# Down projection with four output tiles side by side, gated tiles loaded in pairs, residual loaded later

## The chip, the core and the metric

The kernel runs on one core of one Trainium2 chip, as one program. The metric is the time of the device for one execution, in microseconds (us); a time stands for the median of several runs unless it is said to be that of the profiled execution. The engines are TensorE (PE in the profile; its weight loads are PEld), VectorE (DVE), ScalarE (ACT), GpSimd (POOL) and SyncE (SP). Every DMA of this kernel is issued by SyncE, whose queue takes them in its own order.

## The reference

A trunk of two residual layers over 1024 tokens of width 1024, each a token mixer and a SwiGLU network, and a final norm:

```python
def swiglu(h, w_gate, w_up, w_down):
    return (jax.nn.silu(h @ w_gate) * (h @ w_up)) @ w_down

for layer in range(DEPTH):                       # DEPTH = 2
    i = layer // 2
    hn = rms_norm(h, norm_mix_g[layer])
    if layer % 2 == 0:
        h = h + mixer_ab(hn, ...)
    else:
        h = h + mixer_cd(hn, ...)
    hn = rms_norm(h, norm_ffn_g[layer])
    h = h + swiglu(hn, ffn_w_gate[layer], ffn_w_up[layer], ffn_w_down[layer])
return rms_norm(h, norm_final_g)
```

The hidden width of the SwiGLU is 2816, which is 22 tiles of 128. The change lies in the last product, by w_down, and in the sum with h behind it.

## The kernel before

Everything is kept transposed: features on the 128 partitions, tokens along the free dimension. The tokens are two halves of 512 (HT); the model width is 8 tiles (KT); the hidden width is 22 tiles (NF). Each float32 factor is split into two parts, high and low (split, lines 100 to 103: ScalarE copies the value to float32r for the high part, VectorE subtracts it from the value for the low one), and a product is the sum of three matmuls (mm3, lines 123 to 128): high times high, high times low, low times high.

A unit (line 105) is a split block of 1024 weight columns; there are four of them in a ring, and two buffers (raw) for the loads before the split. The hnp pool has eight buffers of 4 x 512 columns under the tag hn, the hx pool six more. PSUM is divided into two buffers g (psg), three u (psu) and three m (psm), each 128 x 512.

Class Up (lines 246 to 502) computes gate and up for f = 0 to 21 by a scheme with seven products, for both halves in one pass. For each f its products are p1 (operand b11) and p2 (b21) at the start, then p5 (t1), p6 (t2), p7 (t3), and later in end(f) those with t4 and b22. The operands b11, b21, t1 and b22 stand in hnp, and t2, t3 and t4 in hx. Between p1 and p6, ScalarE copies the accumulated tile x out of PSUM (line 326), because p6 goes on accumulating into it; line 348 does the same between p6 and p7, and line 353 between p7 and the t4 product. The finished gated tile of half 0 is stored to DRAM in line 364, that of half 1 in line 372 (hid). The tiles with sums and differences of weights are in a pool of their own ("sums").

Function down (lines 504 to 538) is the down projection. For each half and each of the 8 output tiles d it runs one chain of 22 x 3 matmuls into one PSUM buffer, with weights in three loads of 8, 8 and 6 tiles (line 526). In the first chain of a half, operand(half, f) loads one gated tile (line 516, buffers hr, four of them) and splits it into hx or hnp; the other seven chains read it from there. Behind each chain VectorE adds the result to the residual h (line 537), and after() squares the row for the next norm (piece), stores h in layer 0 (save), and in half 1 starts the norm of half 0: rms behind d = 1, norm or finish behind d = 2. The residual is loaded by begin (line 159), both halves and all 16 tiles, ahead of down (lines 1480 and 1481).

The order on each engine is fixed when the program is built, by a scheduler that works from the program's text and priorities; high_priority moves an instruction ahead. A buffer in a pool is written again when its last readers are done, and the same holds for a new pool that lies on the memory of a closed one. Before, hx is opened once for Up, on top of the pool "sums", and again for down, at the bottom; hr of down lies above it, where Up's t4 was.

Of the kernel before, what the change touches and what calls it, by code (L numbers as in the profile page):

```python
# [9 lines left out]
F32 = mybir.dt.float32  # L10
F32R = mybir.dt.float32r
# [7 lines left out]
P = 128  # L19
# [30 lines left out]


@with_exitstack
def hybrid_trunk_kernel(ctx: ExitStack, tc: tile.TileContext, x_t, w_all, w_down, w_ba, vecs, c_f, c_i, c_rope, out):
    nc = tc.nc
    V, S, G, T = nc.vector, nc.scalar, nc.gpsimd, nc.tensor
    dma = nc.sync.dma_start
# [28 lines left out]
    onesn = const.tile([P, 1], F32, name="onesn")  # L85
    V.memset(onesn, 1.0 / DM)
    mhalf = const.tile([P, 16], F32, name="mhalf")
    V.memset(mhalf, -0.5)

    def psg():  # L90
# [9 lines left out]
    def split(hi, lo, src, eng=V):  # L100

        S.copy(hi, src)  # L102
        eng.tensor_tensor(lo, src, hi.bitcast(F32), op=SUB)  # L103

    def unit():

        return ring.tile([P, 2, DM], F32R, tag="w", name="w", bufs=4)
# [15 lines left out]
    def mm3(o, terms, first=True, last=True, **kw):  # L123
        n = len(terms)
        for i, (lh, ll, rh, rl) in enumerate(terms):
            T.matmul(o, lh, rh, start=first and i == 0, stop=False, **kw)  # L126
            T.matmul(o, lh, rl, start=False, stop=False, **kw)  # L127
            T.matmul(o, ll, rh, start=False, stop=last and i == n - 1, **kw)  # L128
# [19 lines left out]
    class Trunk:  # L148
# [10 lines left out]
        def begin(self, half, src):  # L159

            self.h[half] = [self.hp.tile([P, KH, HT], F32, tag=f"h{half}{i}", name=f"h{half}{i}", bufs=1)
                            for i in range(2)]
            if half == 1:
                self.hp.tile([P, 24], F32, name="pad")
            for d in range(KT):
                dma(self.at(half, d), src[:, d, :])

        def at(self, half, d):
# [77 lines left out]
    class Up:  # L246
# [153 lines left out]

        def turn(self, tr, row, b11, b21, hx, close, left, right):

            self.left.tile([P, 8], F32, name="pad")
# [97 lines left out]
            self.part_d(2, w2, s)  # L501
            return b22, t3, t4

    def down(layer, hid, tr, hx, hr, after):

        slots, n = {}, [0]

        def operand(half, f):

            if f % 2 == 0:  # L510
                n[0] += 1
                p, b = (hx, 6) if n[0] % 14 < 6 else (hnp, 8)
                slots[half, f // 2] = p.tile([P, KH, HT], F32R, tag="hn", name="hidq", bufs=b)
            q = slots[half, f // 2]
            raw = hr.tile([P, HT], F32, tag="hr", name="hr", bufs=4)
            dma(raw, hid[half, f])
            split(q[:, f % 2 * 2, :], q[:, f % 2 * 2 + 1, :], raw)

        for half in range(NH):
            for d in range(KT):  # L520
                o = psu() if d % 2 else psm()
                for f0 in range(0, NF, 8):
                    nf = min(8, NF - f0)
                    w = unit()
                    raw = ring.tile([P, DM], F32, tag="raw", name="raw", bufs=2)
                    dma(raw[:, 0:nf * P], w_down[layer, d, :, f0 * P:(f0 + nf) * P])
                    split(w[:, 0, 0:nf * P], w[:, 1, 0:nf * P], raw[:, 0:nf * P])
                    terms = []
                    for f in range(f0, f0 + nf):
                        if d == 0:  # L530
                            operand(half, f)
                        q, c = slots[half, f // 2], slice((f - f0) * P, (f - f0 + 1) * P)
                        terms.append((w[:, 0, c], w[:, 1, c], q[:, f % 2 * 2, :], q[:, f % 2 * 2 + 1, :]))
                    mm3(o, terms, f0 == 0, f0 + nf == NF)
                h = tr.at(half, d)
                with tc.high_priority(offset=100):
                    V.tensor_tensor(h, h, o, op=ADD)
                after(half, d)


    def out_proj(name, cat_d, tr, src, order, half, hp):
# [902 lines left out]
    for layer in range(2):  # L1444

        mes = ExitStack()
        if layer == 0:
            hp = mes.enter_context(pool("mix"))
            mixer_ab(hn, hp, es.close)
        else:  # L1450
            dg1 = tr.rms(1)
            hp = mes.enter_context(pool("mix"))
            mixer_cd(hn, hp, lambda: hn.append(tr.norm(1, R_MIX + KT, dg1)), es.close)
        es = ExitStack()
        tr = Trunk(es)
# [75 lines left out]
def laid_out(i):  # L1531
# [15 lines left out]
    w_down = np.ascontiguousarray(i["ffn_w_down"].reshape(2, NF, P, KT, P).transpose(0, 3, 2, 1, 4)).reshape(  # L1547
        2, KT, P, NF * P)
# [7 lines left out]
    return [x_t, w_all, w_down, w_ba, np.ascontiguousarray(vecs)] + shape_constants()  # L1556


# [17 lines left out]
```

## Time and profile before

| | |
|---|---|
| three runs, us | 2829.3, 2832.07, 2838.61 |
| median, us | 2832.07 |
| profiled execution: its own time, us | 2837.84 |
| profiled execution: its span, us | 2836.1 |
| mean granted TensorE clock | 0.987 |
| DMA, mean over the span | 110 GB/s |
| down projection, layer 0: half 0, half 1 (us from the span's start) | 1002.8 to 1140.6, 1140.6 to 1264.5 |
| down projection, layer 1: half 0, half 1 | 2556.9 to 2695.0, 2695.0 to 2818.8 |

The profile is of one execution. Its page gives busy times of the engines, the chain of work that ended last (followed back from the last instruction, each step to what released it), groups of instructions and DMA issues. Other views of the trace give the rows of a stretch of time: a timeline (start, length, engine, line, operation, output and inputs, and in brackets how long the engine had been idle and what ended that), busy times by stretches (the length of the stretch, then for each engine busy us and number of instructions, and at the end the granted TensorE clock, the share of the DMA engines and GB/s) and sums of waits (who waited for whom, total, times, longest). In the chain of waits a row "DMA hr<-hid" is a transfer to the tile hr from hid.

### The profile page before, as it was taken

The page shows a single profiled execution, that of the slowest core. Times are in us where ns is not written, and L with a number is a line of the kernel's source. Part 1 is how long each engine was busy: PE and PEld are TensorE (multiplying, and loading weights), DVE is VectorE, ACT ScalarE, POOL GpSimd, SP SyncE. Part 2 cuts the span into 40 slices and gives each one's busy share as a digit, 9 for nine tenths or more (in the row PEclk, how much of TensorE's full clock was granted, in tenths as well). Part 3 has the DMA queues.
Part 4 walks back from the last instruction along what each step waited for, and adds up shares of the span by engine and source line. Part 5 has one row for each costly group of instructions (what it writes and reads, how often), then busy time and mean ns, then how long its engine had stood idle before and what let it go on. Part 6 is the DMA issues. An engine that isn't in the chain of part 4 may idle for free.

```text
span 2836.1 us, 37934 instructions
## 1 busy us (share of the span) xinstructions
PE 2730.9 (96%) x14974; PEld 2227.2 (79%) x14974; DVE 1502.4 (53%) x2599; ACT 1004.7 (35%) x1733; POOL 477.5 (17%) x435
## 2 busy tenths in 40 slices
PE   7999999989999989999999999999998999998998
PEld 5788877768787868889788897887876878876886
DVE  8766555573433343534765756666566334334342
ACT  5432122343333332323444434444434333333221
POOL 0110111333333201010000000000034333320000
PEclk9999999999999999999999999999999999999999
DMA  3334345522222274442132121323742222227442
GB/s 134 107 107 159 91 151 166 166 78 86 82 77 88 82 252 127 142 129 75 46 86 83 57 90 46 86 83 90 244 131 82 83 81 82 75 91 245 123 139 70
DMA packets 166178, 312.82 MB, mean 110 GB/s; under 512 B 22992, under 2 KB 70384, under 8 KB 164848
## 3 DMA queue, kind: packets, MB, share of 16 engines
q1 hardware_dynamic: 166000, 310.40, 34.8%
q8 instruction: 117, 1.92, 0.3%
q14 instruction: 61, 0.50, 0.1%
HBM read 236.32 MB, written 74.01 MB: 109 GB/s over the span
## 4 chain that ended last, share of the span: by engine, by line
PE 78%; DVE 8%; DMA 6%; ACT 4%; issue 3%; POOL 1%; SPq 0%; POOLq 0%; DVEq 0%; ACTq 0%
PE psu L126 17%; PE psu L128 16%; PE psu L127 16%; PE psm L128 4%; PE psm L127 4%; PE psm L126 4%; PE psg L128 3%; PE psg L127 3%; PE psg L126 3%; DMA hr<-hid 1%; DMA raw<-in_dram 1%; DVE w L103 1%; PE psm L1254 1%; DMA cxb<-scr_c 1%; DMA h<-hd 1%
## 5 line engine op out<-in xcount | busy, mean ns | idle before, releaser
L103 DVE TENSOR_TENSOR w<-raw,w 128x1024 fp32r<-128x1024 f32 (+1 forms) x336 | 408.6, 1218 | 610.2 <-ACT w L102 607.7
L102 ACT CAST w<-raw 128x1024 fp32r<-128x1024 f32 (+1 forms) x336 | 327.4, 975 | 649.6 <-PE psm L128 313.4
L126 PE MATMUL psu<-hnh,w 128*128 128x512 f32 x1328 | 532.0, 402 | 3.4 <-ACT w L102 1.9
L127 PE MATMUL psu<-hnl,w 128*128 128x512 f32 x1328 | 526.9, 397 | 0.5 <-DVE hnl L103 0.5
L128 PE MATMUL psu<-hnh,w 128*128 128x512 f32 x1328 | 524.8, 395 | 0.5 <-DVE w L103 0.5
L126 PEld LDWEIGHTS psu<-hnh,w 128*128 128x128 f32 x1328 | 250.7, 189 | 56.7 <-ACT hnh L102 3.5
L128 PEld LDWEIGHTS psu<-hnh,w 128*128 128x128 f32 x1328 | 250.9, 189 | 52.8 <-DVE w L103 1.6
L127 PEld LDWEIGHTS psu<-hnl,w 128*128 128x128 f32 x1328 | 250.7, 189 | 51.9 <-DVE hnl L103 1.9
L182 POOL TENSOR_TENSOR acc<-acc,sq 128x512 f32<-128x512 f32 x48 | 75.5, 1573 | 517.0 <-ACT sq L181 449.8
L126 PE MATMUL psm<-hidq,w 128*128 128x512 f32 x352 | 141.3, 401 | 19.0 <-ACT hidq L102 18.9
L126 PE MATMUL psu<-w,hnh 128*128 128x256 f32 x512 | 149.9, 293 | 0.0
L127 PE MATMUL psu<-w,hnh 128*128 128x256 f32 x512 | 145.3, 284 | 0.0
L128 PE MATMUL psu<-w,hnl 128*128 128x256 f32 x512 | 145.2, 284 | 0.0
L127 PE MATMUL psm<-hidq,w 128*128 128x512 f32 x352 | 141.5, 402 | 2.9 <-DVE hidq L103 2.9
L128 PE MATMUL psm<-hidq,w 128*128 128x512 f32 x352 | 140.1, 398 | 0.0
L126 PE MATMUL psu<-hidq,w 128*128 128x512 f32 x352 | 139.1, 395 | 0.0
L128 PE MATMUL psu<-hidq,w 128*128 128x512 f32 x352 | 138.6, 394 | 0.0
L127 PE MATMUL psu<-hidq,w 128*128 128x512 f32 x352 | 138.3, 393 | 0.0
L295 POOL TENSOR_TENSOR raw<-raw,ws 128x512 f32<-128x512 f32 x40 | 55.8, 1395 | 327.5 <-DVE w L103 327.5
L126 PEld LDWEIGHTS psu<-w,hnh 128*128 128x128 f32 x512 | 98.4, 192 | 0.8 <-issue 0.2
L127 PEld LDWEIGHTS psu<-w,hnh 128*128 128x128 f32 x512 | 98.4, 192 | 0.3 <-issue 0.2
L128 PEld LDWEIGHTS psu<-w,hnl 128*128 128x128 f32 x512 | 98.3, 192 | 0.0
(384 smaller groups left out, 5416.5 us busy)
## 6 DMA issues: line engine op xcount, KB each, us to landing
raw<-in_dram SPq DMA_DIRECT2D x270, 512.0 KB, 3.6
hid<-hid SPq DMA_DIRECT2D x88, 256.0 KB, 2.0
hr<-hid SPq DMA_DIRECT2D x88, 256.0 KB, 3.6
hd<-h SPq DMA_DIRECT2D x48, 256.0 KB, 3.4
raw<-in_dram SPq DMA_DIRECT2D x32, 384.0 KB, 3.1
h<-hd SPq DMA_DIRECT2D x48, 256.0 KB, 6.0
scr_c<-cx SPq DMA_DIRECT2D x8, 1216.0 KB, 4.6
cxb<-scr_c SPq DMA_DIRECT2D x8, 1216.0 KB, 6.0
```

The source lines that it names most:

```text
L102: S.copy(hi, src)
L103: eng.tensor_tensor(lo, src, hi.bitcast(F32), op=SUB)
L126: T.matmul(o, lh, rh, start=first and i == 0, stop=False, **kw)
L127: T.matmul(o, lh, rl, start=False, stop=False, **kw)
L128: T.matmul(o, ll, rh, start=False, stop=last and i == n - 1, **kw)
L182: (eng or (V if d == KT - 1 else G)).tensor_tensor(a, a, q, op=ADD)
L295: G.tensor_tensor(a[:, HT:], a[:, HT:], s[:, :HT], op=SUB)
L1254: T.matmul(o[:, 0:n * P], q[:, j * P:(j + 1) * P], k[:, (j - n + 1) * P:(j + 1) * P], start=True, stop=True)
```

## The change

The first four output tiles of a half are accumulated side by side, in two psu and two psg buffers, by pairs of gated tiles: one pair is loaded by one DMA and split once, and its block of 1024 weight columns (two f, four d; a new array w_four) feeds 24 matmuls. The last four output tiles keep their chains of full depth, from w_down, which now holds these four alone. The residual's tiles are allocated ahead of down, and their loads stand behind the sixth pair of each half in the program's text. hx is opened below "sums" and stays open from Up to the end of down, so its buffers go on rotating; which pool each pair goes to is written out as a string. The norm of half 0 starts behind the second pair of half 1 (rms) and behind its last pair (norm or finish). Two small pads are moved or added. The arithmetic is the same but for the order of the sums.

```diff
-    def down(layer, hid, tr, hx, hr, after):
+    def down(layer, hid, tr, hx, hr, src, step, after):
-        slots, n = {}, [0]
-        def operand(half, f):
-            if f % 2 == 0:
-                n[0] += 1
-                p, b = (hx, 6) if n[0] % 14 < 6 else (hnp, 8)
-                slots[half, f // 2] = p.tile([P, KH, HT], F32R, tag="hn", name="hidq", bufs=b)
+        slots = {}
+        kinds = iter("hhhhxxhhxxx" + "xhhxxxxxhhh")
+        def weights(src, n):
+            w = unit()
+            raw = ring.tile([P, DM], F32, tag="raw", name="raw", bufs=2)
+            dma(raw[:, 0:n], src)
+            split(w[:, 0, 0:n], w[:, 1, 0:n], raw[:, 0:n])
+            return w
+        def operand(half, i):
+            p, b = (hx, 6) if next(kinds) == "x" else (hnp, 8)
+            q = slots[half, i] = p.tile([P, KH, HT], F32R, tag="hn", name="hidq", bufs=b)
+            raw = hr.tile([P, 2, HT], F32, tag="hr", name="hr", bufs=2)
+            dma(raw, hid[half, 2 * i:2 * i + 2].rearrange("f p t -> p f t"))
+            split(q[:, 0:2, :], q[:, 2:4, :], raw)
+        def term(wh, wl, half, f):
             q = slots[half, f // 2]
-            raw = hr.tile([P, HT], F32, tag="hr", name="hr", bufs=4)
-            dma(raw, hid[half, f])
-            split(q[:, f % 2 * 2, :], q[:, f % 2 * 2 + 1, :], raw)
+            return wh, wl, q[:, f % 2, :], q[:, 2 + f % 2, :]
+        def finish(half, d, o):
+            h = tr.at(half, d)
+            with tc.high_priority(offset=100):
+                V.tensor_tensor(h, h, o, op=ADD)
+            after(half, d)
         for half in range(NH):
-            for d in range(KT):
+            os = [psu(), psg(), psu(), psg()]
+            for i in range(NF // 2):
+                operand(half, i)
+                w = weights(w_four[layer, i], DM)
+                v = w.rearrange("p z (f d c) -> p z f d c", f=2, d=4)
+                for d in range(4):
+                    mm3(os[d], [term(v[:, 0, f, d, :], v[:, 1, f, d, :], half, 2 * i + f) for f in range(2)],
+                        i == 0, i == NF // 2 - 1)
+                if i == NF // 4:
+                    tr.load(half, src[half], range(KT))
+                step(half, i)
+            for d in range(4):
+                finish(half, d, os[d])
+            for d in range(4, KT):
                 o = psu() if d % 2 else psm()
                 for f0 in range(0, NF, 8):
                     nf = min(8, NF - f0)
...
+                    w = weights(w_down[layer, d - 4, :, f0 * P:(f0 + nf) * P], nf * P)
+                    mm3(o, [term(w[:, 0, j * P:(j + 1) * P], w[:, 1, j * P:(j + 1) * P], half, f0 + j)
+                            for j in range(nf)], f0 == 0, f0 + nf == NF)
+                finish(half, d, o)
...
+        hes = ExitStack()
         with ExitStack() as fes:
+            hx = hes.enter_context(pool("hx"))
             up = Up(layer, fes.enter_context(pool("sums")))
-            hx = fes.enter_context(pool("hx"))
...
         with ExitStack() as fes:
-            hx = fes.enter_context(pool("hx"))
             tr = Trunk(es)
-            hr = fes.enter_context(pool("hr", side="left"))
+            hr = fes.enter_context(pool("hr"))
             for half in range(NH):
-                tr.begin(half, hd[2 * layer][half])
+                tr.begin(half, None, ())
             def after(half, d):
...
-                if half == 1 and d == 1:
+            def step(half, i):
+                if half == 1 and i == 1:
                     nxt.append(tr.rms(0))
-                if half == 1 and d == 2:
+                if half == 1 and i == NF // 2 - 1:
                     if layer == 0:
                         nxt.append(tr.norm(0, R_MIX + KT, nxt.pop()))
                     else:
                         finish(0, nxt.pop())
-            down(layer, up.hid, tr, hx, hr, after)
+            down(layer, up.hid, tr, hx, hr, hd[2 * layer], step, after)
             if layer == 1:
                 finish(1, tr.rms(1))
+        hes.close()
```

begin takes a range of tiles and calls a new method load, which holds the loop with the DMAs.

More of the change, by code (lines that the diff above doesn't have):

```diff
@@ L52, in hybrid_trunk_kernel @@
 @with_exitstack
-def hybrid_trunk_kernel(ctx: ExitStack, tc: tile.TileContext, x_t, w_all, w_down, w_ba, vecs, c_f, c_i, c_rope, out):
+def hybrid_trunk_kernel(ctx: ExitStack, tc: tile.TileContext, x_t, w_all, w_four, w_down, w_ba, vecs, c_f, c_i, c_rope, out):
     nc = tc.nc
@@ L87, in hybrid_trunk_kernel @@
     mhalf = const.tile([P, 16], F32, name="mhalf")
+    const.tile([P, 8], F32, name="pad")
     V.memset(mhalf, -0.5)
@@ L157, in tmp, with begin @@
             return self.p.tile([P] + list(shape), dt, tag=tag, name=tag, bufs=bufs)
-        def begin(self, half, src):
+        def begin(self, half, src, ds=range(KT)):
             self.h[half] = [self.hp.tile([P, KH, HT], F32, tag=f"h{half}{i}", name=f"h{half}{i}", bufs=1)
@@ L164, in begin, with load @@
                 self.hp.tile([P, 24], F32, name="pad")
-            for d in range(KT):
+            self.load(half, src, ds)
+        def load(self, half, src, ds):
+            for d in ds:
                 dma(self.at(half, d), src[:, d, :])
@@ L401, in turn @@
         def turn(self, tr, row, b11, b21, hx, close, left, right):
-            self.left.tile([P, 8], F32, name="pad")
             for f in range(2):
@@ L523, in down @@
                     nf = min(8, NF - f0)
[L524 to L538, printed above, removed]
+                    w = weights(w_down[layer, d - 4, :, f0 * P:(f0 + nf) * P], nf * P)
+                    mm3(o, [term(w[:, 0, j * P:(j + 1) * P], w[:, 1, j * P:(j + 1) * P], half, f0 + j)
+                            for j in range(nf)], f0 == 0, f0 + nf == NF)
+                finish(half, d, o)
     def out_proj(name, cat_d, tr, src, order, half, hp):
@@ L1545, in laid_out @@
     w_all = np.concatenate(blocks, axis=0)
-    w_down = np.ascontiguousarray(i["ffn_w_down"].reshape(2, NF, P, KT, P).transpose(0, 3, 2, 1, 4)).reshape(
-        2, KT, P, NF * P)
+    down = i["ffn_w_down"]
+    w_four = np.ascontiguousarray(down.reshape(2, NF // 2, 2, P, 2, 4 * P)[..., 0, :].transpose(0, 1, 3, 2, 4)).reshape(
+        2, NF // 2, P, DM)
+    w_down = np.ascontiguousarray(down.reshape(2, NF, P, KT, P).transpose(0, 3, 2, 1, 4)[:, 4:]).reshape(
+        2, 4, P, NF * P)
     x_t = np.ascontiguousarray(i["x"][0].reshape(NH, HT, KT, P).transpose(0, 3, 2, 1))
@@ L1555, in laid_out @@
     vecs = np.concatenate([rows.T, np.broadcast_to(adt, (P, 8))], axis=1)
-    return [x_t, w_all, w_down, w_ba, np.ascontiguousarray(vecs)] + shape_constants()
+    return [x_t, w_all, w_four, w_down, w_ba, np.ascontiguousarray(vecs)] + shape_constants()
 def kernel(**inputs):
```

1 line of the change is left out of this document (removed).

## The prediction

> **What bounds the kernel now.** The page first: TensorE holds the span.
>
> ```profile
> span 2836.1 us, 37934 instructions
> PE 2730.9 (96%) x14974; PEld 2227.2 (79%) x14974; DVE 1502.4 (53%) x2599; ACT 1004.7 (35%) x1733; POOL 477.5 (17%) x435
> PE 78%; DVE 8%; DMA 6%; ACT 4%; issue 3%; POOL 1%; SPq 0%; POOLq 0%; DVEq 0%; ACTq 0%
> ```
>
> The third row is the chain of work that ended last: 78% TensorE, so nothing off TensorE counts unless TensorE waits for it. The change touches the down projection, four equal pieces of work (two layers, two halves, 528 matmuls each). The view by stretches, cut at the end of Up and at the ends of the halves, gives them one row each: layer 0 half 0, layer 1 half 0, layer 0 half 1, layer 1 half 1; in the first column its length.
>
> ```profile
> 1002.80:1140.60 137.80, 126.85 (x529) 99.36 (x528) 56.88 (x68) 48.12 (x68) 11.72 (x7) 0.96 0.62 198
> 2556.90:2695.00 138.10, 127.13 (x530) 100.20 (x529) 57.03 (x68) 48.14 (x68) 11.72 (x7) 0.95 0.58 184
> 1140.60:1264.50 123.90, 123.90 (x539) 100.43 (x538) 52.10 (x64) 37.77 (x49) 11.09 (x8) 1.00 0.40 123
> 2695.00:2818.80 123.80, 123.80 (x539) 100.17 (x537) 41.81 (x48) 28.64 (x36) 10.09 (x7) 1.00 0.33 102
> ```
>
> Both first halves take 14 us more than the second ones, although the second ones also carry the first half's norm matmuls. The timeline of VectorE shows what those cost: its residual adds (line 537) end the chains.
>
> ```profile
> 1064.76 0.69 DVE L537 TENSOR_TENSOR h<-h,psm 128x512 f32<-128x512 f32 x1 [2.21 <-PE psm L128]
> 1079.97 0.69 DVE L537 TENSOR_TENSOR h<-h,psu 128x512 f32<-128x512 f32 x1 [2.21 <-PE psu L128]
> 1156.08 0.69 DVE L537 TENSOR_TENSOR h<-h,psm 128x512 f32<-128x512 f32 x1 [2.25 <-PE psm L128]
> 1171.34 0.69 DVE L537 TENSOR_TENSOR h<-h,psu 128x512 f32<-128x512 f32 x1 [2.26 <-PE psu L128]
> 1187.53 0.69 DVE L537 TENSOR_TENSOR h<-h,psm 128x512 f32<-128x512 f32 x1 [2.25 <-PE psm L128]
> ```
>
> A chain of 66 matmuls takes 15.21 us in half 0 (0.2305 us a matmul) and 15.26 in half 1; with a norm matmul inside, 16.19. Two chains have one, 1.9 us together. So a half costs 123.9 - 1.9 = 122.0 us when nothing is late, and the first halves lose 137.8 - 122.0 = 15.8 and 138.1 - 121.9 = 16.2: **32.0 us in all**. The second halves lose nothing.
>
> Where it goes: TensorE's waits from 1000 to 1060 us and from 2554 to 2612 (total, times, longest), and from the chain of waits between 985 and 1075 us its shares and its longest pieces (start, length).
>
> ```profile
> PE psm L126 <- ACT hidq L102: 9.4, 4, 8.3
> PE psm L126 <- ACT hidq L102: 9.5, 1, 9.5
> by line: DMA hr<-hid 22.9%; DMA h<-hd 13.1%; PE psu L128 8.8%; PE psu L127 8.7%; PE psu L126 8.7%; PE psm L127 6.2%; PE psm L126 6.2%; PE psm L128 5.9%; DVE hidq L103 4.3%; issue 3.0%; ACT hidq L102 2.1%; PE psg L127 2.0%; PE psg L126 2.0%;
> 1002.34 3.24 DMA hr<-hid
> ...
> 1009.27 6.38 DMA h<-hd
> 1015.67 5.37 DMA h<-hd
> 1021.10 5.36 DMA hr<-hid
> ```
>
> TensorE waits for the gated tiles (hidq), and these wait for their loads, which sit behind the residual's (h). The queue (start, length of the issues, count) and the ten-microsecond stretches (last three columns: granted clock, DMA share, GB/s) show why:
>
> ```profile
> 972.04 0.32 SPq L372 DMA_DIRECT2D hid<-hid  x1
> ...
> 996.53 0.37 SPq L516 DMA_DIRECT2D hr<-hid  x1
> ...
> 1008.33 11.02 SPq L166 DMA_DIRECT2D h<-hd  x16
> 1010.00:1020.00 10.00, 7.46 (x29) 5.19 (x29) 4.22 (x5) 3.57 (x5) 0.00 (x0) 0.98 0.96 324
> 1020.00:1030.00 10.00, 4.19 (x9) 3.07 (x10) 2.85 (x5) 3.09 (x5) 0.00 (x0) 0.50 0.98 344
> 1050.00:1060.00 10.00, 10.00 (x44) 8.08 (x44) 4.91 (x6) 3.78 (x5) 1.74 (x1) 1.00 0.90 307
> 2570.00:2580.00 10.00, 0.80 (x4) 0.32 (x2) 1.36 (x2) 1.22 (x2) 0.00 (x0) 0.64 1.04 388
> ```
>
> All 16 residual loads (4.2 MB) go out after eight gated tiles. The DMA engines are full at 324 to 388 GB/s, and the first chain asks for more than that: 22 gated tiles of 256 KB and 1408 KB of weights are 7.2 MB for 15.2 us of matmuls, 474 GB/s. After the long wait the clock is 0.50, so the matmuls that do run are slow too; that is inside the 32.0 us. The Trainium skill ("TensorE: Matmul & The Clock Gate", Part 1) says that TensorE falls to half its clock after about 3.4 us without work and recovers after as much work; the trace agrees, with 0.50 behind a wait of 8.3 us.
>
> **The change, part by part.** *Matmuls.* 2112 before and after, same shapes. Four chains side by side use each pair of gated tiles for 24 matmuls, 24 x 0.2305 = 5.53 us, and the eleven pairs take 60.9 us. The four accumulate in alternating banks; the stretch 1050 to 1060 above, where two chains run interleaved, has 44 matmuls at clock 1.00, like a single chain, so I cost the alternation at nothing.
>
> *Loads.* The first stage now asks for 512 KB of gated tiles and 512 KB of weights per 5.53 us: 190 GB/s instead of 474, and the residual's 2.1 MB per half fits in the rest up to 344 GB/s in 13.6 us. In the instruction order of the changed program the queue issues all eleven pairs of half 0 before the first residual load, which nothing needs until the fourth chain is done 60 us later. The residual of half 1 follows in half 0, too, not in half 1; it has still more time.
>
> *Round trip.* There are two load buffers for pairs, so a buffer must be loaded, cast and subtracted within two pairs, 11.06 us. No 512 KB load of gated tiles is in this trace. Nearest rows: landing times (minimum, median, maximum) of the single tiles, and the weights' loads of the same size; and one cast and one subtraction of 1024 columns.
>
> ```profile
> DMA to landing us min/median/max: 2.5/3.6/5.6
> raw<-in_dram SPq DMA_DIRECT2D x270, 512.0 KB, 3.6
> 965.81 1.05 ACT L102 CAST w<-raw 128x1024 fp32r<-128x1024 f32 x1 [1.61 <-PE psu L128]
> 994.84 1.23 DVE L103 TENSOR_TENSOR w<-raw,w 128x1024 fp32r<-128x1024 f32 x1 [4.27 <-ACT w L102]
> ```
>
> Bounds 3.6 and 5.6 us, since 512 KB alone took 3.6 and the worst small tile 5.6; I take 4.5. The trip is 0.4 + 4.5 + 1.05 + 1.23 = 7.2 us (8.3 at the upper end), under 11.06: covered, and TensorE does not starve. VectorE has 2 x 1.23 = 2.5 us of splits per 5.53, ScalarE 2.1. If this cover were gone, each missing microsecond would cost 44 pairs x 0.5 us.
>
> *The seam to Up.* The load buffers now lie on Up's weight sums, which are free once Up's last weights are split, not on t4, which Up reads until its end. So the first pairs are issued right behind the store at 972.04, not at 996.53, and go into hn tiles whose readers (p1 and p2 of f = 21) end first. The price: in ScalarE's changed order four pair casts and three weight casts stand ahead of Up's last copy of x (line 326), for which the matmuls p6 wait. TensorE's rows, and that copy's:
>
> ```profile
> 979.60 0.39 PE L126 MATMUL psm<-hnh,w 128*128 128x512 f32 x1
> 989.59 0.43 PE psu L126
> 997.18 0.50 PE L126 MATMUL psu<-t4h,w 128*128 128x512 f32 x1 [0.68 <-ACT c L353]
> 970.03 0.57 ACT L326 COPY gt<-psu 128x512 f32<-128x512 f32 x1
> ```
>
> p1 ends at 979.6, and ScalarE casts two pairs until 981.5; the first weight cast waits for p2 and ends at 983.5. The third pair's buffer is free at 981.7 (subtracted), its load lands at 981.7 + 0.5 + 3.6 = 985.8, or 987.8 at 5.6. Cast, weight cast, cast, then a weight cast whose load was issued at 985.1 (landing 988.7 to 990), a Silu and the copy: done at 991.3, or 993.2. p6 began at 989.59 before, and five more t1 matmuls now stand ahead of it, 990.7. So TensorE waits 0.6 to 2.5 us there. In return eleven down matmuls are interleaved behind p6 and behind the t3 matmuls and cover later copies, such as the 0.68 us at 997.18. Net -0.1 to +1.8 us a layer; I take +0.5, **+1.0 for both layers**. After that the first three pairs are split, and the fourth and fifth are 10 us early.
>
> *Ends of the stages.* Four adds fall due at once, 4 x 0.69 = 2.8 us, and in half 1 the norm of half 0 behind them (8 scales and 4 subtractions, 12 x 0.72 = 8.6 us), then the next chain's first weight split, 1.23: 12.6 us. In the changed order all three weight blocks of the fifth chain are split ahead of this, so 15.2 us of matmuls hide it, with 2.6 to spare; layer 1 has 8 scales only. The norm's one-column matmuls move from a chain behind half 0 to two pairs behind, 11.1 us; add, square, two queued splits and the sum are about 5 us, so 6 are to spare. Half 1's fourth pair waits for half 0's last chain, but three pairs, 16.6 us, stand before it. All zero. Four weight blocks fewer and half as many, twice as wide operand splits save VectorE and ScalarE some 15 us off the path: zero.
>
> **Sum.** -32.0 + 1.0 = -31.0 us. The profiled execution took 2837.84 us, 1.74 us around its span of 2836.1; it becomes 2806.8, span 2805.1. It stands 0.2% above the median of the runs, 2832.07; the median becomes **2801**. With the bounds of the seam (-0.2 to +3.6) the change is -32.2 to -28.4, and the three runs spread from 2829.3 to 2838.61, so its own range is 2796 to 2808.
>
> **The rivals.** *The stall shrinks, but half of it stays.* Loads land late in the burst of pairs, residual and weights, and the seam and the first pairs each wait. Against it: the residual stands behind the eleven pairs. For it: the chain's DMA pieces of 5.4 and 6.4 us in such a burst. Half of 32.0 gives 2832 - 16 = 2816; what lies between, 2808 to 2816, is this case.
>
> *No change.* The gain needs the pairs ahead of the residual and ahead of Up's end. If the seam lost 15 us per layer the change would do nothing, 2832; it would need a load at the head of the queue to be late by 13 us more than the bound, and no row shows that.
>
> *Slower: two buffers for pairs are too few.* The place is the four-chain stage, all four times. From a trip of 11.06 us on, landing 8.4 us, each pair lasts half a trip. The residual's loads land in 6.0 us at the median (row below), behind one another. At a landing of 12 us the trip is 14.7, each pair 7.3 instead of 5.53, 1.8 x 44 = 79 us, less 11 for the pairs split early; -31 + 68 gives 2869. It decides from a landing of 10.2 us on, where the loss passes 31.
>
> ```profile
> h<-hd SPq DMA_DIRECT2D x48, 256.0 KB, 6.0
> L126 PE MATMUL psm<-hidq,w x352: 389/392/796, 1002.8 to 2802.9; 128*128 128x512 f32 x176
> ```
>
> *Slower: the clock.* If the bank change every six matmuls made TensorE idle enough to lose its clock, a matmul would cost up to 0.80 instead of 0.39 us (second row, median and maximum). Half clock in a quarter of the four-chain stages, 4 x 60.9 / 4 = 61 us of work, adds 61: 2832 - 31 + 61 = 2862. Against it stands the clock of 1.00 at 1050 to 1060. The Trainium skill ("TensorE: Matmul & The Clock Gate", "A second HAM failure mode: psum-queue depth-cycling") describes such a loss for a kernel that cycles through its banks; by that rule this rival would win, and the stretch at 1050 speaks against it.
>
> **How the numbers follow.** Forecast 0.70, half of the stall 0.17, no change 0.04, two buffers 0.06, clock 0.03. A difference of 0.3% (8.5 us) is about what a measurement of this kernel can tell from none: faster 0.87, within 0.04, slower 0.09. The range reaches down to 2794, for a median at the low end of the runs' spread, and up into the second case, 2815.
>
> **What would show it.** Right: halves 0 within 2 us of 122; no wait for hidq over 3 us; the clock at 1.00 through 1000 to 1060 and 2554 to 2612; gated loads issued from about 972 on; DMA near 200 GB/s there. Wrong: a wait before line 126's t2 matmuls over 3 us (seam), repeated waits of about a microsecond per pair (two buffers), or a clock below 0.9 in the four-chain stage.

## The result, and the profile after

The changed kernel takes 2807.93 us at the median of four runs (2804.58 to 2811.34), the kernel before on the same chip 2831.28 (four runs). The ratio is 0.9913, 95% interval 0.9891 to 0.9935: faster, by about 23 us. Forecast were 2801 us (2794 to 2815) and a gain of 31. In two later comparisons, on other chips and with more runs, the medians lie 27.9 and 28.3 us apart. The profiled execution took 2808.91 us.

From the page of the changed kernel: span, busy time, and the loads of gated tiles (size, median landing).

```profile
span 2806.9 us, 37718 instructions
...
PE 2720.7 (97%) x14974; PEld 2227.2 (79%) x14974; DVE 1492.6 (53%) x2551; ACT 997.1 (36%) x1685; POOL 474.8 (17%) x435
...
hr<-hid SPq DMA_DIRECT2D x44, 512.0 KB, 4.7
```

The matmuls are as many as before, with 10 us less busy time, which fits a mean clock of 0.991 instead of 0.987. The view by stretches of the changed kernel comes next. The first two rows run from the first gated matmul to the end of half 0's last chain, one for each layer, and the others are pieces of the four-chain stage (last three columns: granted clock, DMA share, GB/s).

```profile
997.40:1127.80 130.40, 130.32 (x566) 105.82 (x565) 48.78 (x46) 42.17 (x47) 11.41 (x7) 1.00 0.58 193
2535.00:2665.80 130.80, 130.26 (x566) 105.80 (x565) 48.78 (x45) 41.49 (x46) 11.40 (x7) 1.00 0.54 178
...
1000.00:1060.00 60.00, 60.00 (x262) 48.75 (x262) 25.34 (x22) 19.61 (x21) 1.76 (x1) 1.00 0.73 248
1010.00:1020.00 10.00, 10.00 (x45) 8.10 (x44) 4.48 (x4) 4.69 (x6) 1.76 (x1) 1.00 0.67 215
1020.00:1030.00 10.00, 10.00 (x46) 8.24 (x45) 3.74 (x4) 3.21 (x4) 0.00 (x0) 1.00 0.94 347
1050.00:1060.00 10.00, 10.00 (x45) 8.05 (x44) 2.45 (x2) 2.10 (x2) 0.00 (x0) 1.00 0.22 57
```

The first row holds 566 matmuls, because Up's last ones are now interleaved with the first gated ones. At 0.2305 us each they need 130.5 us, and the stretches are 130.4 and 130.8. Without the 36 matmuls of Up among them that is 122.1 and 122.5 us for the half. So half 0 waits for next to nothing. Before, 529 matmuls (121.9 us) took 137.8. Between 1010 and 1030 the clock was 0.98 and 0.50 before; it is 1.00 now, although the DMA engines are as full as before in the second ten microseconds.

The waits of TensorE in the changed kernel, around the seam of layer 0 and of layer 1 (total, times, longest):

```profile
PE psu L127 <- ACT gt L330: 0.3, 1, 0.3
...
PE psu L127 <- ACT gt L330: 1.6, 1, 1.6
PE psg L127 <- DVE gt L372: 0.5, 1, 0.5
```

No wait for a gated tile is left. Line 330 is line 326 of before, the copy ahead of p6: 0.3 us in one layer, 1.6 in the other. The queue of the changed kernel (start, length of the issues, count) shows why the tiles are there in time:

```profile
975.96 1.14 SPq L525 DMA_DIRECT2D hr<-hid  x2
...
1014.45 0.36 SPq L525 DMA_DIRECT2D hr<-hid  x1
1014.86 1.44 SPq L170 DMA_DIRECT2D h<-hd  x3
```

The first pair is issued at 975.96 instead of 996.53, and the eleventh at 1014.45, just ahead of the first residual load.

To compare runs I use two stretches that hold little but Up and the down projection: from VectorE's last residual add ahead of Up to its last add of the down projection, in each layer. The four rows in the timeline of VectorE, before:

```profile
554.78 0.69 DVE L555 TENSOR_TENSOR h<-h,psg 128x512 f32<-128x512 f32 x1 [2.10 <-PE psg L128]
1264.70 0.69 DVE L537 TENSOR_TENSOR h<-h,psu 128x512 f32<-128x512 f32 x1 [0.70 <-PE psu L128]
2108.70 0.69 DVE L555 TENSOR_TENSOR h<-h,psg 128x512 f32<-128x512 f32 x1 [2.62 <-PE psg L128]
2819.03 0.69 DVE L537 TENSOR_TENSOR h<-h,psu 128x512 f32<-128x512 f32 x1 [14.56 <-PE psu L128]
```

and in the changed kernel:

```profile
557.04 0.69 DVE L576 TENSOR_TENSOR h<-h,psg 128x512 f32<-128x512 f32 x1 [2.35 <-PE psg L129]
1251.30 0.69 DVE L535 TENSOR_TENSOR h<-h,psu 128x512 f32<-128x512 f32 x1 [0.67 <-PE psu L129]
2094.93 0.69 DVE L576 TENSOR_TENSOR h<-h,psg 128x512 f32<-128x512 f32 x1 [2.37 <-PE psg L129]
2789.27 0.69 DVE L535 TENSOR_TENSOR h<-h,psu 128x512 f32<-128x512 f32 x1 [14.53 <-PE psu L129]
```

Before, 709.92 + 710.33 = 1420.3 us; after, 694.26 + 694.34 = 1388.6. The gain in the stretches is 31.7 us, 15.7 and 16.0 by layer. The forecast's parts gave 31.0. The time ahead of Up of layer 0 was 2.3 us longer in this execution (557.04 against 554.78), and that is part of why the whole time shows less.

The stretches hold Up, and Up varies. From the last add ahead of it to the first gated matmul it took 447.5 to 451.0 us in the five profiles of kernels whose gated loads start late (the kernel before twice, and three of the experiments; both layers). So a sum of two stretches is good to a few microseconds, not to tenths.

### The profile page after: what moved, and what is told of

Its sections match the earlier page's. It is cut to its first block, busy times and chain, and to the rows that moved or that the text cites. A ratio compares the mean times of both kernels' runs of the same rounds, so it can differ in the third digit from the quotient of the medians.

```text
span 2806.9 us, 37718 instructions
## 1 busy us (share of the span) xinstructions
PE 2720.7 (97%) x14974; PEld 2227.2 (79%) x14974; DVE 1492.6 (53%) x2551; ACT 997.1 (36%) x1685; POOL 474.8 (17%) x435
## 5 line engine op out<-in xcount | busy, mean ns | idle before, releaser
L104 DVE TENSOR_TENSOR w<-raw,w 128x1024 fp32r<-128x1024 f32 (+2 forms) x332 | 411.4, 1241 | 611.3 <-ACT w L103 610.6
L103 ACT CAST w<-raw 128x1024 fp32r<-128x1024 f32 (+2 forms) x332 | 326.8, 985 | 621.0 <-PE psm L129 238.2
L375 POOL TENSOR_TENSOR hid<-gt,c 128x512 f32<-128x512 f32 x44 | 77.2, 1756 | 138.0 <-ACT gt L373 104.6
L1133 POOL COPY attn<-ac 32x128 f32<-32x128 f32 x32 | 14.0, 436 | 437.7 <-DVE ac L1130 436.7
L284 POOL TENSOR_TENSOR ws<-raw 128x512 f32<-128x512 f32 x42 | 62.9, 1497 | 122.4 <-DVE raw L486 68.2
```

The source lines that it names most:

```text
L284: G.tensor_tensor(s[:, HT:], b[:, :HT], b[:, HT:], op=ADD)
L375: G.tensor_tensor(h, g, self.c22.pop(f), op=MULT)
L1133: G.tensor_copy(attn[z, :, z], ac[z])
```

## The experiments

"Sum" in the table is the sum of the two stretches in the profiled execution, always from the same four rows; the ratio is to the kernel before on the same chip.

| kernel | median us | ratio (95%) | sum us |
|---|---|---|---|
| before, again | 2835.64 | 0.9999 (0.9987 to 1.0011) | 1421.6 |
| residual late alone | 2816.25 | 0.9922 (0.9901 to 0.9942) | 1401.9 |
| four chains alone | 2821.78 | 0.9948 (0.9932 to 0.9963) | 1403.2 |
| early loads alone | 2804.28 | 0.9893 (0.9878 to 0.9908) | 1387.1 |
| early loads, residual late | 2805.77 | 0.9899 (0.9884 to 0.9914) | 1387.1 |
| the same, two single buffers | 2816.94 | 0.9930 (0.9915 to 0.9944) | 1403.0 |
| four chains, residual late, loads after Up | 2809.75 | 0.9913 (0.9899 to 0.9928) | 1389.3 |
| changed, residual first in the program | 2807.41 | 0.9893 (0.9875 to 0.9911) | 1393.0 |
| changed, one pair buffer | 2805.22 | 0.9898 (0.9881 to 0.9914) | 1384.7 |
| the same again | 2805.68 | 0.9886 (0.9868 to 0.9903) | 1388.2 |
| changed, second | 2808.18 | 0.9891 (0.9871 to 0.9910) | 1388.7 |
| changed, third | 2807.45 | 0.9897 (0.9882 to 0.9912) | 1390.3 |

**Where the missing microseconds are.** The kernel before and the changed kernel, each unaltered, on one chip.

> The kernel before, unchanged, with a second profile. Theory A (the first halves of the down projection lose 15.8 and 16.2 us in every execution, and the changed kernel's missing 8 us are variation between executions elsewhere, such as the 0.5 clock after waits at the start of Up): first halves of 138 us each within 0.5, ratio 1.00 within 0.3%, and the stretch from 520 to 635 us moves by up to 3 us against the first profile. Theory B (the profiled execution of before was slow in the down projection itself, and the stall is normally shorter): first halves of 133 to 136 us. Theory C (the shared hx pool costs 3 us at the start of Up): 520 to 635 us within 0.3 us of the first profile.

> The changed kernel, unchanged, with a second profile. Theory A: the 3.2 us that were lost between 523 and 631 us change by a microsecond or more, the first halves stay within 0.5 us of 122 from the end of Up. Theory C: the 3.2 us stay within 0.3. Ratio 0.991, within 0.3%.

The stretches repeat within 2 us, 1420.3 and 1421.6 before, 1388.6, 1388.7 and 1390.3 in the changed kernel, so the two lie 30 to 33 us apart. What repeats less well is the time ahead of Up. The last add ahead of Up of layer 0 came at 551.1 us in the repeat of before and at 549.3 in that of the changed kernel, against 554.78 and 557.04 above. The stretch 510 to 520 us by its granted clock, in before, in the changed kernel and in its repeat:

```profile
510.00:520.00 10.00, 10.00 (x43) 8.20 (x42) 4.72 (x4) 2.74 (x3) 1.13 (x1) 0.95 0.58 206
```

```profile
510.00:520.00 10.00, 10.00 (x36) 8.03 (x35) 5.86 (x5) 3.33 (x4) 2.22 (x1) 0.77 0.65 208
```

```profile
510.00:520.00 10.00, 10.00 (x50) 8.39 (x49) 5.33 (x7) 4.32 (x5) 2.04 (x2) 1.00 0.58 155
```

Much the same part of the program (the executions are up to 8 us apart there) ran at 0.95, 0.77 and 1.00, with 43, 36 and 50 matmuls in ten microseconds. Theory A holds in the main: the gain is in the stretches in every pair of profiles, and the time outside them varies by as much as the first comparison lacked. One of its numbers was missed. From the first gated matmul to the last add of half 0, the repeat of the kernel before took 139.7 and 138.5 us, the first profile 139.9 and 140.2; in layer 1 that is 1.7 us less, not within 0.5. Theory C, a lasting cost of the new layout at Up's start, falls: the stretches hold that start, and they shrank by all that the stall had cost.

**Residual late alone.** In the kernel before:

```diff
-                tr.begin(half, hd[2 * layer][half])
+                tr.begin(half, None, ())
...
+                if d == 0:
+                    tr.load(half, src[half], range(KT))
                 h = tr.at(half, d)
```

> The kernel before with the residual's loads of each half moved behind its first chain in the text, nothing else. If the residual's 4.2 MB in front of the gated tiles are the main part of the stall: the first chain's 7.2 MB at 344 GB/s take 21 us instead of 15.2, the loss falls from 16 to 5 to 7 us a layer, ratio 0.993. If the demand of the first chain alone (474 GB/s and the round trip of four small buffers) sets it: the loss stays at 12 us or more, ratio 0.997.

It earns 18.4 to 19.7 us of the stretches (against 1420.3 and 1421.6), and 19.8 us between the medians, where the changed kernel earns 27.9 on the same chip. The sum puts it low, because Up took 451.0 and 449.9 us here, and 448.0 and 448.2 in the first profile of the kernel before. Its half 0 by stretches, layer 0 and layer 1, and its queue:

```profile
1003.00:1129.40 126.40, 124.62 (x530) 98.19 (x529) 57.61 (x69) 49.02 (x69) 11.29 (x7) 1.00 0.67 217
2547.50:2674.30 126.80, 124.18 (x530) 98.36 (x529) 58.28 (x69) 48.85 (x69) 11.53 (x7) 1.00 0.64 201
...
1006.64 2.61 SPq L519 DMA_DIRECT2D hr<-hid  x4
1009.30 0.42 SPq L169 DMA_DIRECT2D h<-hd  x1
1011.38 2.90 SPq L519 DMA_DIRECT2D hr<-hid  x4
1014.32 1.37 SPq L169 DMA_DIRECT2D h<-hd  x3
```

530 matmuls need 122.2 us, so 4.2 and 4.6 us are still lost in the first halves, where 15.8 and 16.2 were lost before: 23.2 of the 32.0 us are earned, some seven tenths, as by the medians. The first reading of the expectation holds. The clock is 1.00: the long wait is gone, and with it the half clock behind it. In the queue the residual does not stand behind the chain, though its loads do in the text: they go out one to three at a time between fours of gated tiles. So the run shows what it earns to spread the burst of sixteen, not what a queue without the residual would earn.

**Residual first in the changed kernel's program.** The changed kernel with the loads back at their old place in the text:

```diff
-                tr.begin(half, None, ())
+                tr.begin(half, hd[2 * layer][half])
...
-                if i == NF // 4:
-                    tr.load(half, src[half], range(KT))
```

> The changed kernel with all 16 residual loads ahead of the down projection in the text, as before. The scheduler still puts them behind the eleven pairs of half 0 in the queue. If that order is what counts: first halves within 0.5 us of the changed kernel's, ratio 0.991. If the 16 loads in one burst (4.2 MB, 12 us at 344 GB/s) delay the weights of pairs 7 to 10: a wait of 1 to 4 us per layer, ratio 0.993.

No difference in the time. The residual's tiles lie on memory that Up still holds, and its loads stand behind all eleven pairs in the queue of either program. The run does not test the residual's place, only that this line of the change does nothing while the others are there. Its sum, 1393.0, is 3 to 4 us above the other profiles of the changed kernel, and that lies in Up: from the last add to the first gated matmul it took 442.2 and 443.0 us, in the others 439.9 to 441.4. The sixteen loads in one burst cost TensorE no wait.

**Early loads alone.** The kernel before with the memory layout of the change, and nothing else:

```diff
+        hes = ExitStack()
         with ExitStack() as fes:
+            hx = hes.enter_context(pool("hx"))
             up = Up(layer, fes.enter_context(pool("sums")))
-            hx = fes.enter_context(pool("hx"))
...
-            hx = fes.enter_context(pool("hx"))
             tr = Trunk(es)
-            hr = fes.enter_context(pool("hr", side="left"))
+            hr = fes.enter_context(pool("hr"))
...
-                n[0] += 1
-                p, b = (hx, 6) if n[0] % 14 < 6 else (hnp, 8)
+                p, b = (hx, 6) if next(kinds) == "x" else (hnp, 8)
```

> The kernel before with one part of the change: the load buffers lie on Up's weight sums and six of the fourteen gated tiles come from the pool that Up shares, so the gated loads may start before Up's end. Loads stay single (256 KB, four buffers), the down projection stays chain after chain, and the residual's 32 loads stay ahead of it in the program; in the queue of the instruction order 18 of the 22 gated loads of half 0 then stand ahead of the residual's. Theory A (it is the place in the queue that costs the 32 us: whoever stands ahead of the residual earns most of it): 14 to 20 us under the kernel before, 2816 to 2822 against 2836, since the last four gated tiles still wait behind 4.2 MB (about 12 us less the lead). Theory B (the first chain asks for too many bytes in 15 us, and only four chains side by side mend that): a gain of 8 us or less, 2828 to 2836, with waits for gated tiles of over 5 us. By theory C of the seam (ScalarE's casts ahead of Up's last copy delay it) the wait before the last Up matmuls grows by 1 to 2 us here too.

This alone gives the whole gain: 2804.28 us, sum 1387.1, 33 to 34 us under before. That is below what either theory named. The expectation had miscounted the queue, which in the profile of this kernel stands so:

```profile
971.48 0.61 SPq L515 DMA_DIRECT2D hr<-hid  x1
...
1008.72 2.11 SPq L515 DMA_DIRECT2D hr<-hid  x3
1010.89 0.42 SPq L167 DMA_DIRECT2D h<-hd  x1
```

The residual's tiles lie on memory that Up holds to its end, and its loads go out at 1010.89 us, about where they did before (1008.33). With a head start of 25 us all 22 gated loads of half 0 and four of half 1 go out ahead of it. Half 0 by stretches, both layers:

```profile
993.30:1123.30 130.00, 130.00 (x566) 105.88 (x565) 50.40 (x60) 43.51 (x61) 11.45 (x7) 1.00 0.60 191
2532.10:2662.20 130.10, 130.10 (x566) 105.93 (x566) 50.96 (x61) 43.66 (x61) 11.44 (x7) 1.00 0.57 178
```

TensorE is busy in all of it, with chains one after the other and single loads. The rate of 474 GB/s, on which the forecast built the need for four chains, is what the first chain asks for when no tile is there yet; here twelve of the 22 loads had been issued before the first gated matmul (993.3 us). The run does not part the head start from the place in the queue: with the one comes the other. The seam's wait was 0.7 and 0.5 us here, so theory C's 1 to 2 us more did not come.

**Early loads and late residual, single chains.** The two edits together.

> The early gated loads and the late residual together, with the chains one after the other and single loads as before: all of the change but the four chains and the pairs. Theory A (queue order and an early start are the whole gain; with some eleven tiles loaded ahead, the first chain asks for 4.3 MB in 15.2 us, 283 GB/s, which the queue gives): 2804 to 2811, the same as the changed kernel (2807.5) within 4 us, first halves of 122 to 124 us. Theory B (four chains are needed, since 7.2 MB in 15.2 us are more than the 344 GB/s that were seen): as the late residual alone or a little under it, 2813 to 2818, with waits for gated tiles of 3 to 5 us per layer.

2805.77 us, sum 1387.1: the same again. Theory A, in its numbers.

**Four chains without the early start.** The changed kernel with the layout edits above undone, so hx is opened anew behind Up and the load buffers lie on t4 again; the residual stays late.

> The changed kernel with the load buffers back on the tensor that Up reads to its end, and the gated tiles' pool opened behind Up, so that no gated load starts before Up's last matmuls (about 996 us instead of 972); four chains and pairs stay. Theory A (with four chains a pair lasts 5.53 us, so the start costs one trip of 7.2 us less the 6 us of Up that are left, and the seam's own price of 0.5 to 2 us is saved): 2805 to 2812, no difference to the changed kernel that can be measured. Theory B (the early start is what fills the first pairs; without it the first two come 4 to 6 us late in each layer and the clock falls): 2816 to 2825.

Half 0 by stretches:

```profile
1004.90:1127.80 122.90, 122.19 (x530) 99.16 (x529) 53.48 (x48) 44.55 (x48) 11.15 (x7) 1.00 0.66 216
2543.40:2666.30 122.90, 122.18 (x530) 99.16 (x529) 53.50 (x48) 44.41 (x48) 11.14 (x7) 1.00 0.61 199
```

122.9 us for 530 matmuls: 0.7 lost. Sum 1389.3. So four chains with the residual late also earn most of it without a head start: 24.9 us by the medians, where the early loads alone earn 30.3 on the same chip. Here too the residual's loads go out between the pairs, one to three at a time from 1009.01 us on. Either cure nearly suffices, and together they earn no more than the early loads alone.

**Four chains alone.** The same with the residual ahead of the down projection in the program.

> The kernel of the run with four chains and late gated loads, with the residual's 32 loads put ahead of the down projection in the program as in the kernel before: four chains and pairs alone, without the early start and without the late residual. In the instruction order three pairs stand ahead of all sixteen residual loads of a half. Theory A (four chains cut the rate that the loads must keep to 190 GB/s, so three pairs, 16.6 us of matmuls, cover most of the 12 us that the residual holds the queue): pair 4 comes 3 to 6 us late in each layer, 2814 to 2822 in all, and both layers' stretch from the last add ahead of Up to the last add of the down projection together 1396 to 1404 us (before 1420 and 1422, changed kernel 1388.6 and 1388.7). Theory B (the gain of four chains hangs on the residual standing behind them): the residual's 12 us show in full, the stretches together 1412 or more, 2826 to 2836. Theory C (the queue holds nothing up): no difference to the changed kernel, 2804 to 2812.

The queue, the waits around the seams (layer 0, then layer 1), and the stretches of this kernel:

```profile
1009.21 0.38 SPq L525 DMA_DIRECT2D hr<-hid  x1
1009.68 10.20 SPq L169 DMA_DIRECT2D h<-hd  x16
1020.28 1.05 SPq L525 DMA_DIRECT2D hr<-hid  x2
```

```profile
PE psu L126 <- ACT hidq L102: 3.6, 1, 3.6
...
PE psu L126 <- ACT hidq L102: 5.4, 1, 5.4
```

```profile
1005.60:1134.80 129.20, 124.33 (x530) 100.20 (x529) 53.50 (x48) 44.60 (x48) 11.18 (x7) 0.99 0.63 206
2548.20:2678.50 130.30, 124.15 (x530) 99.97 (x529) 53.51 (x48) 44.79 (x48) 11.12 (x7) 0.97 0.58 189
...
1020.00:1030.00 10.00, 5.84 (x22) 4.04 (x21) 3.04 (x3) 3.03 (x3) 0.00 (x0) 0.95 0.94 351
```

Here is the stall that the forecast described, cut in half: pair 4 is issued at 1020.28 behind sixteen residual loads, TensorE waits 3.6 and 5.4 us for it, and the clock falls: to 0.95 and, in the next ten microseconds, 0.88; in layer 1 to 0.74 from 2570 to 2580. Half 0 takes 7.0 and 8.1 us more than its matmuls need. The sum of 1403.2 and the 2821.78 us fit theory A. The Trainium skill ("TensorE: Matmul & The Clock Gate", Part 1) puts the loss of the clock at about 3.4 us without work; both waits are over that, and the trace agrees in so far as the clock is below 1.00 behind them. A shorter wait can do it, too, as the run with two single buffers below shows (0.83 behind a wait of 2.1 us).

**One pair buffer.** The changed kernel with one edit:

```diff
-            raw = hr.tile([P, 2, HT], F32, tag="hr", name="hr", bufs=2)
+            raw = hr.tile([P, 2, HT], F32, tag="hr", name="hr", bufs=1)
```

> The changed kernel with one load buffer for pairs instead of two: each load waits until the pair before it is cast and subtracted, so the distance between two issues in the four-chain stage is the round trip itself. Theory A (the trip is 7.2 to 8.3 us, as forecast from the parts): issues 7.2 to 9 us apart; with three pairs split ahead, a stage of eleven pairs takes 8 trips and one pair, 63 to 77 us instead of 60.9, so 2816 to 2872 in all, 2835 at a trip of 7.7. Theory B (the trip is near 11 us, and two buffers only just suffice): issues over 10 us apart, 88 us a stage, 2900 and more. Theory C (landing and splits overlap so well that the trip is under 6.5): no measurable loss, 2804 to 2812.

No loss. The queue of this kernel in the four-chain stage:

```profile
1018.35 0.37 SPq L525 DMA_DIRECT2D hr<-hid  x1
...
1025.07 0.37 SPq L525 DMA_DIRECT2D hr<-hid  x1
...
1031.42 0.37 SPq L525 DMA_DIRECT2D hr<-hid  x1
...
1039.52 0.37 SPq L525 DMA_DIRECT2D hr<-hid  x1
...
1046.11 0.37 SPq L525 DMA_DIRECT2D hr<-hid  x1
```

The round trip is 6.4 to 8.1 us, with the residual in the queue between. That is longer than the 5.53 us that a pair lasts, but the stage ends before the lag has eaten the head start: the rows are those of pairs 7 to 11, and the matmuls of the eleventh begin at 1060.20 us, 14 us behind its issue. The expectation had counted three pairs as split ahead; by the first gated matmul (999.6 us) four were issued, and Up's last 24 matmuls add time. The second run of this kernel, beside the changed one, asked whether its lower sum was real:

> The changed kernel with one pair buffer again, now on the same chip as the changed kernel. Theory A (with one buffer fewer pair casts stand ahead of the last copy of Up, and the seam is shorter by 1 to 2 us a layer): 2 to 4 us under the changed kernel of this call, the two stretches together 1384 to 1387 us. Theory B (the 4 us between their profiles were chance): within 2 us of it, 1388 to 1390.

> The changed kernel itself for the third time, beside the one with one pair buffer. It was 2807.93 and 2808.18 us at the median; expected 2805 to 2811, ratio to the kernel before 0.989 to 0.991 (forecast from the parts: 31 us, 0.9891), the two stretches together 1388 to 1394 us.

Sums of 1388.2 and 1390.3, means of 2804.3 and 2807.3 us over five runs each, with a spread of 5 to 10 us: 3 us that these runs cannot tell from chance; the sum is theory B's. One buffer is enough; that it is faster is open.

**The same bytes under way, single chains.** The run with early loads and late residual, with two single buffers instead of four, so 512 KB under way as with one pair buffer.

> The early loads and the late residual with the chains one after the other, as in the run of that kind, but with two single load buffers instead of four: 512 KB of gated tiles under way at a time, as in the run with one pair buffer and four chains, which lost nothing. Theory A (what a chain of the first kind needs is a lead times a rate, and four chains are what makes a low rate do): two tiles per round trip of 5.3 to 6.2 us, so 22 tiles from 972 us on take 58 to 68 us and end at 1030 to 1040, where the first chain ended at 1019 with four buffers: 12 to 20 us lost per layer, 2830 to 2846. Theory B (the early start alone is what counts, whatever the rate): no more than 4 us per layer lost, 2804 to 2813.

Half 0 by stretches, layer 0 and layer 1, then half 1, and ten microseconds of half 0 in layer 1 with the only wait of TensorE from 2545 to 2565 us:

```profile
997.00:1127.90 130.90, 128.49 (x554) 103.09 (x553) 50.74 (x59) 41.94 (x57) 11.45 (x7) 1.00 0.58 185
2539.00:2671.00 132.00, 129.60 (x554) 104.50 (x553) 51.25 (x59) 42.31 (x58) 11.71 (x7) 0.99 0.54 169
...
1128.20:1253.60 125.40, 124.79 (x538) 99.02 (x537) 54.81 (x69) 41.14 (x54) 11.30 (x8) 1.00 0.44 135
2671.00:2799.40 128.40, 126.36 (x538) 100.42 (x536) 44.73 (x52) 32.12 (x41) 11.09 (x7) 0.99 0.36 114
...
2560.00:2570.00 10.00, 10.00 (x38) 7.97 (x37) 4.42 (x7) 3.89 (x7) 0.00 (x0) 0.83 0.75 245
PE psm L127 <- ACT hidq L103: 2.1, 1, 2.1
```

2816.94 us lies between the two theories' numbers. The sum is 1403.0, 16 us above the same kernel with four buffers, 8 per layer where theory A had 12 to 20. With these buffers TensorE waits in half 0: 554 matmuls need 127.7 us, so 3.2 and 4.3 are lost there. The rest is in half 1, which takes 125.4 and 128.4 us, and 122.3 and 123.0 with four buffers: 3.1 and 5.4 more. By the medians, each against the kernel before on its own chip, the two kernels lie 10 us apart (gains of 18.9 and 28.8). So this is what four chains do: with 512 KB under way they lose nothing, and single chains lose 10 to 16 us. The two also differ in the size of a load, one of 512 KB against two of 256 KB; no run parts that from the order of the chains.

## Why the prediction was right, point by point

**The stall** (32.0 us): right in size and place. Half 0 now needs what its matmuls need, and the stretches shrank by 30 to 33 us. **The seam** (+0.5 a layer, wait of 0.6 to 2.5): 0.3 and 1.6 us waited, the first below the forecast's bound, and 0.8 to 1.3 in the two later profiles; stall less gain leaves 0.1 and 0.2 us net, which is less than Up varies by. **The ends of the stages** (zero): right, the second halves take 122.4 and 121.9 us from add to add, and took 122.0 and 121.9. **Edits at zero**: alternating the banks costs nothing. 262 matmuls ran from 1000 to 1060 us at clock 1.00, one per 0.229 us. The rule of the Trainium skill ("TensorE: Matmul & The Clock Gate", "A second HAM failure mode: psum-queue depth-cycling"), by which the clock rival would have won, does not show with a bank change every six matmuls. **The round trip**: landing 4.7 us (forecast 4.5), and two buffers are more than needed.

**Luck in the zero for the banks.** The forecast drew it, and its case against the clock rival, from the stretch 1050 to 1060, "where two chains run interleaved". They do not run there: in the trace, all 66 matmuls from 1049.34 to 1064.33 us go to psm, those of one chain. Two chains did run interleaved ahead of it, to 1045.5, by one to eleven matmuls at a time and with short waits between:

```profile
1030.00:1045.00 15.00, 14.17 (x58) 10.01 (x56) 7.57 (x11) 6.88 (x11) 0.00 (x0) 1.00 0.72 236
```

The clock is 1.00 there, so this row would have carried the argument; the one that was named could not. Three smaller slips changed nothing. The copy shown at 970.03 us is not Up's last one, which ran at 988.89. The forecast's own range, 2796 to 2808, does not come out of its terms: 2829.3 - 32.2 and 2838.61 - 28.4 are 2797.1 and 2810.2. The landing from which two buffers would have lost 31 us is 10.3 us, not 10.2.

**The cause** was only half right. The forecast laid the stall on the rate, 474 GB/s, and on the residual's place in the queue. Both matter, but so does the start: with the loads begun at 971 us, the same chains and the same order in the program cost nothing. The early start, which the forecast put down as a price at the seam with the first pairs split ahead in return, earns the 32 us alone; four chains with the late residual are another cure, which earns most of it. The sum came out right because the change holds both, and the early start alone is enough; that was luck. The edit that does it alone, where the load buffers and the shared pool lie, is not even among the three that the title names.

**The time**: 2807.93 instead of 2801, 7 us. It lies at the edge between two of the forecast's cases, since from 2808 us on half of the stall was to be left; the time alone does not tell them apart, but the rows do, with no wait for a gated tile. The term that was mis-sized is the base from which the 31 us were taken. The three runs shown had their median at 2832.07; three later groups of runs of the same kernel had 2834.61, 2835.79 and 2836.07. Less 31.0 these give 2803.6 to 2805.1, and the changed kernel ran at 2807.45 to 2808.18. The 3 us that remain are within what the time ahead of Up varies by (549.3 to 557.0 us in the three profiles of the changed kernel, 551.1 and 554.8 in the two of the kernel before); whether a small part of them is lasting stays open.

**What would show it**: halves within 2 us, no wait for a gated tile, clock at 1.00, first load at 975.96 (972 and the 2.3 us of the later start of Up make 974.3): all right. "DMA near 200 GB/s" was wrong: 215 to 347 from 1010 to 1030 and 57 from 1050 on, because the residual and the first pairs of half 1 follow close behind the eleventh pair.

## What to carry to other kernels

When an engine starves at the start of a stage, ask first how early its loads may be issued, that is, whose memory their buffers lie on; a change of pool order earned here as much as the rewritten loop order and more. A loop that uses each load more often lowers the rate that the loads must keep, and pays where buffers are few: with 512 KB under way it saved 10 to 16 us, with 1 MB nothing. Two cures of one stall do not add up, so price each alone before keeping both.

## What the runs showed of the hardware

The landing of the same 512 KB load of gated tiles was 4.7 us at the median with two buffers and 3.8 with one, beside 3.6 for weights of that size; what makes the difference was not tried apart. Sixteen residual loads of 256 KB took 10.20 us to issue in one kernel and 11.02 in the kernel before. Behind waits of 3.6 and 5.4 us the clock fell below 1.00, and once behind a wait of 2.1 us (0.83 over ten microseconds). The time from the start to the last add ahead of Up of layer 0 was 549.3 to 558.0 us over the profiles of all these kernels.
